# Modulation sums in PSUM: 14 instead of 5 of 24 blocks on VectorE, weight-tile halves split by VectorE and GpSimd, forget logits by chunk

## The chip, the cores and the metric

The kernel runs on one core of one Trainium2 chip. Times are device microseconds (us) of one execution of the whole program; ns is said where it is meant. Engines are called TensorE (matmuls), VectorE, ScalarE, GpSimd and SyncE (which issues the large loads). In rows of the profile they are PE (and PEld for weight loads), DVE, ACT, POOL and SP.

## What is computed

One layer of a hybrid encoder trunk, 256 positions of width 2048, batch 1. Cut to what the change touches:

```
mod = SiLU(c) @ W_ada + b_ada          # 6 sections of 2048 numbers: shift, scale, gate, twice
h   = RMSNorm(x) * (1 + scale_1) + shift_1
z   = h @ W_in                         # 5120 columns and 8 of the forget gates
y_A = gated MLP;  y_B = trailing means minus identity (windows 2, 4, 8, 16)
y_C = forgetting attention (8 heads x 128)
x   = x + gate_1 * (concat[y_A, y_B, y_C] @ W_out)
h   = RMSNorm(x) * (1 + scale_2) + shift_2
x   = x + gate_2 * MoE(h)              # 16 experts, top 1 group, top 2 experts
```

All of it is in float32. c is one vector, so mod is one row of 6 x 2048 numbers, each a sum over 2048 rows of W_ada.

## The kernel before

**Chunks and stages.** The width 2048 is 16 blocks k of 128. h and its share of z = h @ W_in are made chunk by chunk, CHUNKS = [(0, 2), (2, 2), (4, 4), (8, 4), (12, 4)], each (first block, number of blocks). A chunk is a stage: stage 0 runs from about 26 to 61 us of the profiled execution, stage 1 to 102, stage 2 to 169, stage 3 to 236 and stage 4 to 372. In a stage all columns of W_in are taken for the chunk's rows; the first chunk's result is copied into z (ScalarE, line 436), the later ones' are added to it (VectorE, line 438). Stage 4 has, between its nine weight tiles, the mixers too (gated MLP, trailing means, attention). From 372 to 501 us follows the output projection, four column blocks of W_out of 512 columns; after it come routing and the experts, to the end.

**Weight tiles.** Weights come as tiles of 1 MB through a ring of six, loaded by SyncE in the order in which the code asks for them; a step's load and its preparation are issued up to two steps (LOOK) ahead of its matmuls. W_in and W_out tiles are used in halves of 128x1024: ScalarE casts a half to a reduced type (hi, line 174), VectorE or GpSimd subtracts to get the rest (lo, line 175), and both go into one of three buffers whl. TensorE then does 24 matmuls for a half (hi by hi, lo by hi, hi by lo). A tile's result fills two of three PSUM banks pm, so the add into z must empty them soon. WSPLIT names the engine that splits the second half of a tile in each stage (the first is always VectorE's), WSO the same for W_out.

**Modulation blocks.** After the first chunk's, 24 blocks of mod are left: shift_1 and scale_1 for four chunks (M1A, M1B), shift and scale of the second sublayer (M2A, M2B), gate_1 (G1) and gate_2, four each. A block is 16 k rows by 256 or 512 columns of W_ada: two ring tiles or four, four k rows (eight at 256 columns) in a tile. There are two ways. With "P" TensorE multiplies one column of SiLU(c) by the tile, 16 matmuls in fp32 into a PSUM bank ada (ada_parts); a copy to SBUF and a few one-column matmuls then turn the row. With "V" (sum_parts) VectorE accumulates 16 products into an SBUF tile (ga, or grow for the gates), lines 290 and 292, and TensorE adds over the partitions afterwards with ones.

**Order.** The schedule is written by hand. PLAN has one list for each of the stages 0 to 3, one string for each weight tile: "n" asks for the next ring tile of the next chunk's modulation, "m" for one of the second sublayer's, a digit finishes a block (its column sums), "h" makes the next chunk's h (make_h). LAST is the same for stage 4. Stage 0 has besides band(g), which builds four masks for the trailing means, with VectorE (minimum, reciprocal at line 371, comparisons) and GpSimd (iota, products at lines 373 to 378). make_h needs the chunk's shift and scale, and stands at the end of the stage before. It also makes the forget gates' logits: per block k one matmul over the fp32 rows hf into a PSUM bank (late), the last of them after the first half-product.

Of the kernel before, what the change touches and what calls it, by code (L numbers as in the profile page):

```python
# [22 lines left out]
KD = D // 128  # L23
# [10 lines left out]
for _n, _w in (("c", 16), ("bcol", 64), ("gmix", 16), ("gffn", 16), ("wfz", 128), ("bs", 4), ("bscale", 4), ("qg", 1),  # L34
# [22 lines left out]
    ["n", "n", "n", "n0", "1h"],  # L57
    ["nnn", "n", "0n", "nnn", "1h"],
# [9 lines left out]
M1A, M1B, M2A, M2B, G1 = "PPVV", "PPPP", "PPPP", "PPPP", "PVVV"  # L68
WSPLIT, WSO = "VGGGG", "G"
# [46 lines left out]
def body(tc, x_d, prm_d, bg_d, wada_d, win_d, wout_d, egu_d, ed_d, out_d):  # L116
# [155 lines left out]
    def sum_parts(sec, k0, nk, after, eng, tile_of, bias=None):  # L272
        r = 16 // nk
        ng = KD // r
        buf = []

        def one(g):
            def prep():
                w = ada_load(sec, k0, nk, g)
                if g == 0:  # L280
                    buf.append(tile_of()[:, :128 * nk])
                return w
# [83 lines left out]
    def band(g):  # L366
        w = (2, 4, 8, 16)[g]
        rc = wk.tile([128, T], F32, name="hf")
        G.iota(rc, pattern=[[1, 256]], base=1, channel_multiplier=0, allow_small_or_imprecise_dtypes=True)
        V.tensor_scalar(rc, rc, float(w), None, op0=OP.min)  # L370
        V.reciprocal(rc, rc)
        V.scalar_tensor_tensor(rc, jp, float(w), rc, op0=OP.is_lt, op1=OP.mult)
        G.tensor_tensor(band0[:, g, :], rc, tri, op=OP.mult)
        G.tensor_tensor(band0[:, g, :128], band0[:, g, :128], ident, op=OP.subtract)
        rc = wk.tile([128, T], F32, name="hf")
# [68 lines left out]
    WS = [{"V": V, "G": G}[c] for c in WSPLIT]  # L444

    def piece(q, name):
# [8 lines left out]
        halves(win_d, WIN[q, c0], (V, WS[q]), lambda c, h: hpart(q, c, h), banks, True, True,  # L455
               lambda P: put(q, c0, P))

    def small_piece(q, c0, n):
        buf = []

        def one(a):
            def prep():
# [5 lines left out]
                split(hl[:, 0], hl[:, 1], buf[0][:, :, 512 * a:512 * a + 512], (V, WS[q])[a])  # L468
# [14 lines left out]
    def col_mod(sec, i, chunk, gain=None, eng=None):  # L483
# [15 lines left out]
        return steps(sum_parts(sec, k0, nk, after_sum, eng, lambda: wk.tile([128, 512], F32, name="ga", bufs=2)))  # L499
# [12 lines left out]
    def forget_a():  # L512
        fs = wk.tile([128, 256], F32, name="hf")
# [137 lines left out]
    def pool_mix():  # L651
        bsc = par("bscale")
        ds_ = []
        for g in range(5):
            if g < 4:
# [4 lines left out]
                d = wk.tile([128, 256], F32, name="hf")  # L660
# [159 lines left out]
    WO = (V, {"V": V, "G": G}[WSO])  # L820
# [67 lines left out]
    def g1_steps(n):  # L888
# [6 lines left out]
        return steps(sum_parts(2, 4 * n, 4, lambda a: None, ENG(G1[n]), lambda: r4s[n], n))  # L895
# [509 lines left out]
```

## Time and profile before

| | |
|---|---|
| median of 3 runs | 1456.18 us (1456.14 to 1457.46) |
| the profiled execution | 1460.89 us, its span 1459.1 us |
| mean granted TensorE clock | 0.958 |
| TensorE busy | 1264.6 us, 87% of the span |
| VectorE busy | 693.5 us, 48% |
| ScalarE busy | 412.8 us, 28% |
| GpSimd busy | 146.0 us, 10% |
| moved by DMA | 539.14 MB, 369 GB/s |

The span is what the trace covers, 1.8 us less than the execution's own time. Busy shares are means over stages that differ: GpSimd's 146 us all lie in the first 501 us. In rows of groups, `xN` is the number of instructions, then come the busy time in us and the mean of one in ns, then the idle time of the engine just ahead of them and what ended most of it. In rows of the timeline the first number is the start, the second the length, and brackets say how long the engine had been idle and for what.

### The profile page before, as it was taken

What the parts mean: (1) busy time and instruction counts of PE and PEld (TensorE: products, weight loads), DVE (VectorE), ACT (ScalarE), POOL (GpSimd) and SP (SyncE); (2) the same over time, 40 slices, a digit from 0 to 9 for tenths busy, and PEclk for the clock granted to TensorE, in tenths of its full rate; (3) what the DMA queues carried; (4) which work ended last, traced back from release to release, by engine and by line L of the source; (5) the groups of instructions that cost most, each with busy time, mean ns of one, the idle gap of its engine ahead of it and who ended that gap; (6) DMA issues with size and microseconds to landing.
All of it is one profiled execution on the core that took longest, in us unless ns stands there. A gap on an engine that the chain in (4) does not pass through costs nothing.

```text
span 1459.1 us, 17581 instructions
## 1 busy us (share of the span) xinstructions
PE 1264.6 (87%) x6930; PEld 703.1 (48%) x6930; DVE 693.5 (48%) x1184; ACT 412.8 (28%) x720; POOL 146.0 (10%) x89
## 2 busy tenths in 40 slices
PE   5999999999989997999968999789997879858865
PEld 3666666666667563575324753337633222222221
DVE  3757483555798372795125961169711202202112
ACT  4433333646333240583003840028400000000000
POOL 0423332311333100000000000000000000000000
PEclk8999999999999998999999999999999999979988
DMA  9787787888877868998999989999899999999997
GB/s 378 270 348 281 281 340 265 303 351 328 349 278 270 310 288 367 427 428 317 421 426 427 426 318 419 424 428 426 333 408 428 427 426 427 428 426 428 426 426 303
DMA packets 49207, 539.14 MB, mean 369 GB/s; under 512 B 5464, under 2 KB 5592, under 8 KB 7008
## 3 DMA queue, kind: packets, MB, share of 16 engines
q1 hardware_dynamic: 47664, 534.79, 89.7%
q10 hardware_dynamic: 1456, 3.17, 0.6%
q8 instruction: 56, 0.92, 0.2%
q14 instruction: 31, 0.25, 0.0%
HBM read 535.85 MB, written 2.10 MB: 369 GB/s over the span
## 4 chain that ended last, share of the span: by engine, by line
PE 38%; DMA 27%; DVE 5%; issue 1%; ACT 1%; DVEq 0%; ACTq 0%
PE lbank L170 28%; DMA ring<-in_e_down_dram 11%; DMA ringl<-in_e_gu_dram 9%; DMA ring<-in_e_gu_dram 7%; PE bank L170 5%; PE pm L170 3%; DVE grow L292 2%; PE ada L170 1%; DVE whl L175 1%; DVE el L175 1%; ACT el L174 0%; DVE grow L290 0%; PE lgp L170 0%; DVE hid L1225 0%; PE pt L170 0%
## 5 line engine op out<-in xcount | busy, mean ns | idle before, releaser
L170 PE MATMUL pm<-whl,hT 128*128 128x512 f32 x1120 | 300.9, 405 | 19.9 <-DVE whl L175 10.8
L170 PEld LDWEIGHTS pm<-whl,hT 128*128 128x128 f32 x1120 | 212.3, 193 | 93.6 <-issue 15.3
L170 PE MATMUL lbank<-ringl,xr 128*32 128x256 f32 (+1 forms) x1152 | 143.7, 496 | 38.0 <-DMA ringl<-in_e_gu_dram 37.8
L170 PE MATMUL lbank<-el,xs 128*128 128x512 f32 x576 | 139.9, 401 | 10.2 <-ACT el L174 7.4
L170 PE MATMUL lbank<-ring,xr 128*32 128x256 f32 (+1 forms) x864 | 105.6, 491 | 34.1 <-DMA ring<-in_e_gu_dram 34.0
L174 ACT CAST whl<-ring 128x1024 fp32r<-128x1024 f32 x96 | 99.0, 1048 | 125.7 <-PE pm L170 70.7
L175 POOL TENSOR_TENSOR whl<-ring,whl 128x1024 fp32r<-128x1024 f32 x43 | 108.3, 2518 | 231.7 <-ACT whl L174 211.0
L170 PEld LDWEIGHTS lbank<-el,xs 128*128 128x128 f32 x576 | 109.3, 192 | 41.0 <-ACT el L174 10.6
L170 PE MATMUL bank<-y,gt 128*128 128x512 f32 x240 | 119.1, 619 | 0.0
L1284 DVE TENSOR_TENSOR xa<-xa,bank 128x512 f32<-128x512 f32 x120 | 82.5, 687 | 69.9 <-PE bank L170 69.9
L170 PEld LDWEIGHTS lbank<-ringl,xr 128*32 128x32 f32 (+1 forms) x1152 | 51.9, 128 | 129.8 <-issue 68.5
L170 PE MATMUL lbank<-ring,hidT 128*64 128x512 f32 (+1 forms) x576 | 103.8, 624 | 11.5 <-DMA ring<-in_e_down_dram 11.5
L1275 DVE TENSOR_TENSOR y<-lbank,g2w 128x512 f32<-128x512 f32 x60 | 41.5, 691 | 145.7 <-PE lbank L170 145.7
L174 ACT CAST el<-ring 128x512 fp32r<-128x512 f32 x144 | 89.7, 623 | 29.6 <-PE lbank L170 21.7
L175 DVE TENSOR_TENSOR el<-ring,el 128x512 fp32r<-128x512 f32 x144 | 92.7, 688 | 0.0
L175 DVE TENSOR_TENSOR whl<-ring,whl 128x1024 fp32r<-128x1024 f32 x53 | 72.2, 1368 | 35.9 <-ACT whl L174 33.6
L170 PE MATMUL ada<-ring,cact 128*1 128x512 f32 (+1 forms) x648 | 75.1, 566 | 15.6 <-DMA ring<-in_w_ada_dram 14.4
L1171 ACT COPY gt<-bank 128x256 f32<-128x256 f32 x15 | 5.6, 372 | 287.9 <-PE bank L1169 287.9
L170 PEld LDWEIGHTS lbank<-ring,xr 128*32 128x32 f32 (+1 forms) x864 | 39.5, 128 | 98.4 <-DMA ring<-in_e_gu_dram 48.4
L1225 DVE TENSOR_TENSOR hid<-hid,lbank 128x512 f32<-128x512 f32 x12 | 8.2, 687 | 165.0 <-PE lbank L170 164.7
L170 PE MATMUL lbank<-el,hidT 128*128 128x512 f32 x288 | 74.8, 411 | 12.2 <-DVE el L175 8.3
L438 DVE TENSOR_TENSOR z<-z,pm 128x512 f32<-128x512 f32 x72 | 49.0, 685 | 71.8 <-PE pm L170 71.8
(363 smaller groups left out, 1219.3 us busy)
## 6 DMA issues: line engine op xcount, KB each, us to landing
ringl<-in_e_gu_dram SPq DMA_DIRECT2D x60, 2048.0 KB, 20.1
ring<-in_w_ada_dram SPq DMA_DIRECT2D x90, 1024.0 KB, 7.0
ring<-in_e_gu_dram SPq DMA_DIRECT2D x45, 2048.0 KB, 24.4
ring<-in_e_down_dram SPq DMA_DIRECT2D x45, 2048.0 KB, 25.6
ring<-in_w_in_dram SPq DMA_DIRECT2D x35, 1024.0 KB, 7.0
ringm<-in_e_gu_dram SPq DMA_DIRECT2D x15, 2048.0 KB, 21.7
ringm<-in_e_down_dram SPq DMA_DIRECT2D x15, 2048.0 KB, 21.5
ring<-in_w_out_dram SPq DMA_DIRECT2D x12, 1024.0 KB, 8.3
```

The costliest lines, as they stand in the source:

```text
L170: E.matmul(out, lhsT=lhsT, rhs=rhs, start=start, stop=stop, skip_group_check=True)
L174: S.copy(hi, src)
L175: (eng or V).tensor_tensor(lo, src, hi.bitcast(F32), op=OP.subtract)
L292: eng.scalar_tensor_tensor(a, w[:, j, :], ck, a, op0=OP.mult, op1=OP.add)
L438: V.tensor_tensor(dst, dst, P[h], op=OP.add)
L1171: S.copy(gt, p[:, :256])
L1225: V.tensor_tensor(hid[:, o], hid[:, o], P[2 * b + 1], op=OP.mult)
L1275: V.tensor_tensor(y, P, g2w[:, c0:c0 + 512], op=OP.mult)
L1284: V.tensor_tensor(a, a, p, op=OP.add)
```

## The change

Nine more blocks go from "P" to "V": shift_1 and scale_1 for chunk 1, scale_1 for chunks 3 and 4, the second sublayer's shift entirely, and shift_1 for chunk 2 (of 24 blocks 14 are then VectorE's, two of the nine are 256 columns wide). The partial sums now lie in the PSUM bank ada that the "P" way uses; only the last of 16 operations writes to an SBUF tile. Every first half of a weight tile is split by VectorE and every second half by GpSimd; before, this held everywhere but in stage 0, where VectorE did both. The forget logits of a chunk are all issued behind the first half-product. The tile hf gets five buffers instead of two, and PLAN asks for the next chunk's modulation earlier.

```diff
@@
 PLAN = [
-    ["n", "n", "n", "n0", "1h"],
-    ["nnn", "n", "0n", "nnn", "1h"],
+    ["nn", "nn", "0", "", "1h"],
+    ["nn", "nn", "nn0", "nn", "1h"],
     ["n", "n", "nm", "nn", "n", "n", "n", "0m", "1h"],
     ["mn", "n", "n", "n", "n", "nn", "n0", "m", "1h"],
 ]
@@
-M1A, M1B, M2A, M2B, G1 = "PPVV", "PPPP", "PPPP", "PPPP", "PVVV"
-WSPLIT, WSO = "VGGGG", "G"
+M1A, M1B, M2A, M2B, G1 = "VVVV", "VPVV", "VVVV", "PPPP", "PVVV"
+WSPLIT, WSO = ["VG", "VG", "VG", "VG", "VG"], "VG"
@@
-    def sum_parts(sec, k0, nk, after, eng, tile_of, bias=None):
+    def sum_parts(sec, k0, nk, after, acc, eng, tile_of, bias=None):
         r = 16 // nk
         ng = KD // r
+        P = accs[acc][:, :128 * nk]
...
             def run(w):
-                a = buf[0]
                 for j in range(r):
                     k = r * g + j
                     ck = cact[:, k:k + 1]
                     if k == 0:
-                        eng.tensor_scalar(a, w[:, j, :], ck, None, op0=OP.mult)
+                        eng.tensor_scalar(P, w[:, j, :], ck, None, op0=OP.mult)
+                    elif k < KD - 1:
+                        eng.scalar_tensor_tensor(P, w[:, j, :], ck, P, op0=OP.mult, op1=OP.add)
                     else:
-                        eng.scalar_tensor_tensor(a, w[:, j, :], ck, a, op0=OP.mult, op1=OP.add)
+                        a = tile_of()[:, :128 * nk]
+                        eng.scalar_tensor_tensor(a, w[:, j, :], ck, P, op0=OP.mult, op1=OP.add)
@@
-        rc = wk.tile([128, T], F32, name="hf")
+        rc = wk.tile([128, T], F32, name="hf", bufs=5)
@@ def make_h(q):
-            if late is not None:
-                late()
-
-            def late(k=k, t=t):
+            ts.append((k, t))
+
+        def late():
+            for k, t in ts:
                 o = 32 * (k % 4)
                 mm(fzp[o:o + 8, :], wfz[:, k, :], t, start=k < 4, stop=k >= KD - 4)
         todo.insert(1, (late, None, False)) if todo else late()
@@
-    WS = [{"V": V, "G": G}[c] for c in WSPLIT]
+    WS = [[{"V": V, "G": G}[c] for c in x] for x in WSPLIT]
```

How this moves instructions is seen in the program's order on VectorE and GpSimd. Names are those of the tiles (out<-in), L175 is the split, and xN stands for N alike in a row; line numbers are each kernel's own (L287 and L289 of the changed kernel are the sums in PSUM).

VectorE in stage 0 before, from its first weight tile on: both halves of two ring tiles, then a band's four operations, then splits again.

```order
L175 TENSOR_TENSOR whl<-ring_65,whl 128x1024 x2
L175 TENSOR_TENSOR whl<-ring_63,whl 128x1024 x2
L370 TENSOR_SCALAR hf<-hf 128x256
L371 RECIPROCAL hf<-hf 128x256
L372 SCALAR_TENSOR_TENSOR hf<-jp,hf 128x256
L376 TENSOR_SCALAR hf<-jp 128x128
L175 TENSOR_TENSOR whl<-ring_64,whl 128x1024 x2
```

The same place after:

```order
L175 TENSOR_TENSOR whl<-ring_65,whl 128x1024
L175 TENSOR_TENSOR whl<-ring_63,whl 128x1024
L370 TENSOR_SCALAR hf<-hf 128x256
L371 RECIPROCAL hf<-hf 128x256
L372 SCALAR_TENSOR_TENSOR hf<-jp,hf 128x256
L376 TENSOR_SCALAR hf<-jp 128x128
L287 TENSOR_SCALAR ada_108<-ring_65,cact 128x256
L289 SCALAR_TENSOR_TENSOR ada_108<-ring_65,cact,ada_108 128x256 x7
L289 SCALAR_TENSOR_TENSOR ada_108<-ring_63,cact,ada_108 128x256 x7
L292 SCALAR_TENSOR_TENSOR ga<-ring_63,cact,ada_108 128x256
L175 TENSOR_TENSOR whl<-ring_65,whl 128x1024
```

The second halves have left VectorE, and the 16 operations of a block stand between a band and the next split.

GpSimd in stage 0 after, from the first second half on (before, the four bands' rows stood in a row here, and no split of stage 0):

```order
L175 TENSOR_TENSOR whl<-ring_65,whl 128x1024
L369 IOTA hf 128x256
L373 TENSOR_TENSOR band_134<-hf,tri 128x256
L374 TENSOR_TENSOR band_134<-band_134,ident 128x128
L377 TENSOR_TENSOR band_135<-hf,tri 128x128
L378 TENSOR_TENSOR band_135<-band_135,ident 128x128
L175 TENSOR_TENSOR whl<-ring_63,whl 128x1024
```

A second half's split now stands behind a band's four products on GpSimd.

VectorE in stage 4 before, around the first half of the seventh weight tile: the split follows ylo (a gated MLP result) directly.

```order
L175 TENSOR_TENSOR ylo<-pt_114,hT_124 128x256
L175 TENSOR_TENSOR whl<-ring_63,whl 128x1024
L324 TENSOR_TENSOR mod<-ada_108,prm_69 128x4
L325 SCALAR_TENSOR_TENSOR mod<-mod,prm_69 128x4
L438 TENSOR_TENSOR z<-z,pm 128x512 x2
```

The same place after:

```order
L175 TENSOR_TENSOR ylo<-pt_114,hT_124 128x256
L287 TENSOR_SCALAR ada_109<-ring_65,cact 128x512
L289 SCALAR_TENSOR_TENSOR ada_109<-ring_65,cact,ada_109 128x512 x3
L175 TENSOR_TENSOR whl<-ring_63,whl 128x1024
L324 TENSOR_TENSOR mod<-ada_108,prm_69 128x4
L325 SCALAR_TENSOR_TENSOR mod<-mod,prm_69 128x4
L289 SCALAR_TENSOR_TENSOR ada_109<-ring_65,cact,ada_109 128x512 x4
L289 SCALAR_TENSOR_TENSOR ada_109<-ring_63,cact,ada_109 128x512 x4
L438 TENSOR_TENSOR z<-z,pm 128x512 x2
```

One tile's sum of a second-sublayer block stands ahead of the split now, two more ahead of the adds into z.

## Rows read from the trace of the kernel before

**Rows 1.** Windows: length; busy PE, PEld, DVE, ACT, POOL (count); granted clock, DMA share, GB/s.

```profile
26.00:61.00 35.00, 32.73 (x183) 23.35 (x182) 24.54 (x31) 21.19 (x32) 10.01 (x16) 0.95 0.86 326
61.00:102.00 41.00, 39.48 (x203) 25.14 (x204) 21.71 (x30) 11.12 (x13) 14.82 (x9) 0.96 0.75 292
...
236.00:372.00 136.00, 131.47 (x783) 85.11 (x782) 72.44 (x173) 72.42 (x194) 29.69 (x22) 0.99 0.80 304
372.00:501.00 129.00, 117.60 (x569) 88.80 (x568) 92.66 (x87) 43.80 (x62) 45.46 (x20) 0.95 0.78 299
501.00:1459.00 958.00, 805.24 (x4510) 386.01 (x4510) 390.12 (x726) 212.52 (x361) 0.00 (x0) 0.95 0.96 401
```

**Rows 2.** Timeline of TensorE in stage 2: start, length, operation.

```profile
147.40 1.04 PE L170 MATMUL ada<-ring,cact 128*1 128x512 f32 x8
148.37 5.73 PE L170 MATMUL pm<-whl,hT 128*128 128x512 f32 x24
```

**Rows 3.** Groups of VectorE over the whole program, forms apart.

```profile
L175 DVE TENSOR_TENSOR whl<-ring,whl 128x1024 fp32r<-128x1024 f32 x53 | 72.2, 1368 | 35.9 <-ACT whl L174 33.6 <-POOL whl L175 2.2
...
L438 DVE TENSOR_TENSOR z<-z,pm 128x512 f32<-128x512 f32 x72 | 49.0, 685 | 71.8 <-PE pm L170 71.8
...
L292 DVE SCALAR_TENSOR_TENSOR grow<-ring,cact,grow 128x512 f32<-128x512 f32 x33 | 35.3, 1069 | 1.0
...
L585 DVE SCALAR_TENSOR_TENSOR s<-pt,Fq,maskb 128x256 f32<-128x256 f32 x5 | 2.4, 476 | 0.0
```

**Rows 4.** Timeline of VectorE and GpSimd in the output projection.

```profile
417.29 3.10 DVE L292 SCALAR_TENSOR_TENSOR grow<-ring,cact,grow 128x512 f32<-128x512 f32 x4
...
421.15 3.20 POOL L175 TENSOR_TENSOR whl<-ringm,whl 128x1024 fp32r<-128x1024 f32 x1 [5.46 <-ACT whl L174]
...
422.04 5.22 DVE L292 SCALAR_TENSOR_TENSOR grow<-ring,cact,grow 128x512 f32<-128x512 f32 x4
```

**Rows 5.** TensorE's waits, 372 to 470 us, and its timeline around them.

```profile
PE pm L170 <- DVE xg L839: 7.0, 3, 3.1
...
404.39 0.50 PE L170 MATMUL pm<-whl,hT 128*128 128x512 f32 x1 [1.27 <-DVE xg L839]
...
434.87 0.72 PE L170 MATMUL pm<-whl,hT 128*128 128x512 f32 x1 [2.70 <-DVE xg L839]
435.39 0.63 PE L170 MATMUL pm<-whl,ylo 128*128 128x512 f32 x1
...
438.86 0.39 PE L170 MATMUL pm<-whl,ylo 128*128 128x512 f32 x1
```

**Rows 6.** Timeline of stage 0 on ScalarE, VectorE and TensorE.

```profile
35.26 0.58 ACT L436 COPY z<-pm 128x512 f32<-128x512 f32 x1 [0.72 <-PE pm L170]
...
38.28 1.75 DVE L371 RECIPROCAL hf<-hf 128x256 f32<-128x256 f32 x1
...
40.07 0.42 DVE L372 SCALAR_TENSOR_TENSOR hf<-jp,hf 128x256 f32<-128x256 f32 x1
...
60.89 1.16 PE L170 MATMUL pt<-diag,xa 128*128 128x128 f32 x8 [0.96 <-DVE mod L320]
```

**Rows 7.** GpSimd: a split in the timeline of stage 2, and the bands' groups.

```profile
152.55 2.40 POOL L175 TENSOR_TENSOR whl<-ring,whl 128x1024 fp32r<-128x1024 f32 x1 [4.23 <-ACT whl L174]
...
L374 POOL TENSOR_TENSOR band<-band,ident 128x128 f32<-128x128 f32 x4 | 4.4, 1106 | 0.3
...
L373 POOL TENSOR_TENSOR band<-hf,tri 128x256 f32<-128x256 f32 x4 | 2.9, 734 | 24.6 <-DVE hf L372 24.6
```

**Rows 8.** VectorE's waits, 236 to 372 us (total us, times, longest), and its timeline.

```profile
DVE z L438 <- PE pm L170: 21.1, 13, 4.4
...
DVE qk L571 <- ACT qk L570: 6.6, 6, 4.2
...
245.51 0.69 DVE L438 TENSOR_TENSOR z<-z,pm 128x512 f32<-128x512 f32 x1 [3.52 <-PE pm L170]
...
256.84 0.69 DVE L438 TENSOR_TENSOR z<-z,pm 128x512 f32<-128x512 f32 x1 [4.38 <-PE pm L170]
```

More of the change, by code (lines that the diff above doesn't have):

```diff
@@ L278, in prep @@
             def prep():
[L279 to L282, printed above, removed]
+                return ada_load(sec, k0, nk, g)
             def run(w):
-                a = buf[0]
                 for j in range(r):
@@ L374, in band @@
         G.tensor_tensor(band0[:, g, :128], band0[:, g, :128], ident, op=OP.subtract)
-        rc = wk.tile([128, T], F32, name="hf")
+        rc = wk.tile([128, T], F32, name="hf", bufs=5)
         V.tensor_scalar(rc[:, :128], jp[:, :128], float(w), 1.0 / w, op0=OP.is_lt, op1=OP.mult)
@@ L388, in make_h @@
         hq = hbuf(q)
-        late = None
+        ts = []
         for c in range(nk):
@@ L394, in make_h @@
                 mm(p[:, 128 * h:128 * h + 128], xa[:, h, 128 * k:128 * k + 128], diag[:, h, :])
-            t = wk.tile([128, T], F32, name="hf")
+            t = wk.tile([128, T], F32, name="hf", bufs=5)
             V.tensor_scalar(t, p[:, :T], mod[:, 1, k:k + 1], mod[:, 0, k:k + 1], op0=OP.mult, op1=OP.add)
             split(hq[:, 0, c, :], hq[:, 1, c, :], t)
-            if late is not None:
-                late()
-            def late(k=k, t=t):
+            ts.append((k, t))
+        def late():
+            for k, t in ts:
                 o = 32 * (k % 4)
@@ L453, in banks @@
             return P
-        halves(win_d, WIN[q, c0], (V, WS[q]), lambda c, h: hpart(q, c, h), banks, True, True,
+        halves(win_d, WIN[q, c0], WS[q], lambda c, h: hpart(q, c, h), banks, True, True,
                lambda P: put(q, c0, P))
@@ L467, in prep @@
                 hl = hp.tile([128, 2, 2, 512], F32R, name="whl")
-                split(hl[:, 0], hl[:, 1], buf[0][:, :, 512 * a:512 * a + 512], (V, WS[q])[a])
+                split(hl[:, 0], hl[:, 1], buf[0][:, :, 512 * a:512 * a + 512], WS[q][a])
                 return hl
@@ L498, in col_mod @@
             return steps(ada_parts(sec, k0, nk, after, 0 if sec < 2 else 1))
-        return steps(sum_parts(sec, k0, nk, after_sum, eng, lambda: wk.tile([128, 512], F32, name="ga", bufs=2)))
+        return steps(sum_parts(sec, k0, nk, after_sum, 0 if sec < 2 else 1, eng, lambda: wk.tile([128, 512], F32, name="ga", bufs=2)))
     for f in col_mod(0, 0, CHUNKS[0]) + col_mod(1, 1, CHUNKS[0], "gmix"):
@@ L512, in forget_a @@
     def forget_a():
-        fs = wk.tile([128, 256], F32, name="hf")
+        fs = wk.tile([128, 256], F32, name="hf", bufs=5)
         V.tensor_copy(fs, fzp)
@@ L659, in pool_mix @@
                 mm(p[:, 128:256], z[:, 1, c0:c0 + 128], band1[:, g, :], start=False)
-                d = wk.tile([128, 256], F32, name="hf")
+                d = wk.tile([128, 256], F32, name="hf", bufs=5)
                 V.tensor_copy(d, p[:, :256])
@@ L818, in body @@
     V.tensor_scalar(limR, capR, -1.0, 512.0, op0=OP.mult, op1=OP.add)
-    WO = (V, {"V": V, "G": G}[WSO])
+    WO = [{"V": V, "G": G}[c] for c in WSO]
     def wout_steps(n, Ps):
@@ L894, in g1_steps @@
             return steps(ada_parts(*gate_args(2, n, r4s[n])))
-        return steps(sum_parts(2, 4 * n, 4, lambda a: None, ENG(G1[n]), lambda: r4s[n], n))
+        return steps(sum_parts(2, 4 * n, 4, lambda a: None, n % 2, ENG(G1[n]), lambda: r4s[n], n))
     r4s = []
```

## Prediction, made before the changed kernel ran

> **What bounds the kernel now.** I read the busy time by stage first [rows 1]. In the five chunk stages (26 to 372 us) TensorE is busy 93 to 97% of the time (stage 0: 32.73 of 35 us; stage 4: 131.47 of 136), while VectorE has between 10 and 64 us free per stage. In the stretch from 372 to 501 us, the output projection, TensorE drops to 117.60 of 129. After 501 us come routing and experts; nothing there is edited, and it begins when the part before it is done. So the change is worth what it moves the end of the first 501 us; the last 958 us are carried along.
>
> TensorE's rhythm in a chunk stage is seen in the timeline [rows 2]: 24 matmuls of a weight tile take 5.73 us, and one tile of a modulation block 1.04 us, overlapping its neighbours by some 0.07. Two other readings matter. The accumulator sum of a block that VectorE does already runs at 3.10 us for 4 operations when nothing disturbs it, 0.775 us each, and at 5.22 us for 4 when GpSimd's split of a weight tile runs at the same moment [rows 4]. And at the boundary between two column blocks of the output projection TensorE stands 2.70 us behind VectorE; over three such boundaries 7.0 us [rows 5].
>
> **The change, step by step.**
>
> *Price of one sum operation in PSUM.* The trace has no accumulation into PSUM. Nearest rows [rows 3]: a 512-wide add with one PSUM input takes 685 ns (z adds, 72 of them), with nothing that depends on it next: the lower bound, 0.69. A 256-wide scalar_tensor_tensor takes 476 ns with a PSUM input and 0.42 without [rows 3, 6], so PSUM adds 0.05. On 0.775 this gives 0.83 us, which I take: 3.3 us for a tile of 4, and 0.56 for the 256-wide operations of stage 0. Upper bound: the mean of the present sums with GpSimd's blocking in it, 1069 ns [rows 3], if PSUM does not free them of it. That it does is my reading of the 72 z adds: their mean equals an undisturbed add, though GpSimd works in the same stages; the splits without a PSUM operand average 1368 ns.
>
> The Trainium skill says the same in "SBUF — State Buffer", Who interferes with whom: the pair of SBUF ports that VectorE shares with GpSimd is locked for a whole instruction, and a VectorE instruction with at most one SBUF input, outside the two-port modes, doesn't need it. The trace agrees (5.22 against 3.10 for two SBUF inputs, 685 ns for one); by this rule the sums cost no more than the undisturbed price.
> Against the change speaks "Perfetto Trace Analysis", Optimizing Scalar/DVE Operations: an access costs VectorE about 60 ns in SBUF and 125 in PSUM. By that an operation would take 0.84 instead of 0.83 (an estimate from that page), and the total below would rise by 1 to 2 us; the 0.05 us of the rows is a little less.
>
> *What TensorE loses.* Nine more blocks leave it: seven with 4 tiles of about 0.95 us, two with 2 tiles of 1.04, together 31 us. That is the gain if nothing else becomes late.
>
> *Stage 0.* It gets both 256-wide blocks: 32 operations of 0.56 us, 18 us. VectorE had 10 us free, and gives 5 us of splits to GpSimd. But its order is now fixed as split, band, 16 sums, split, band, 16 sums, split, split. The first split of this chain follows ScalarE's cast, which now stands behind all four copies of the first tile (the last copy ended at 35.26 + 0.6 [rows 6]): it runs from 36.9 to 38.1. Then band 2.7 (the 1.75 us reciprocal is most of it [rows 6]), sums 9.0, split 1.2, band 2.7, sums 9.0, split 1.2: 63.9 us. Only now is the first half of the fourth tile ready, and three halves of 2.9 us remain for TensorE: 72.6, then column sums. Before, the stage's h began at 60.89 [rows 6]. **+12 us.** On GpSimd each second half's split now stands behind four band products (0.73, 1.1 and two smaller ones) that wait for VectorE's reciprocal, and takes 2.40 us itself [rows 7]: the second tile's second half is ready only at about 45, the third's at 58. TensorE waits there too, but these waits lie inside the VectorE chain just counted.
>
> *Stage 1.* Eight sums (6.6 us) now stand between a tile's split and the adds that empty its PSUM banks; with three banks TensorE can start just one more half-product. A cycle is split 1.2, sums 6.6, add 0.7, product 1.45, add 0.7: 10.7 us for a tile that took about 7. Two such tiles, +8, less 4 us of modulation matmuls: **+4**.
>
> *Stages 2 and 3.* Nine tiles, ten sum tiles each. A tile costs VectorE 1.2 + 1.4 + 3.3 = 5.9 us against TensorE's 5.73; two tiles carry a double sum (9.2). The gain of 5 to 6 us of modulation matmuls, of the 1 us that the forget matmuls no longer stand ahead of the first product, and of two present waits is eaten by these: **-1** together.
>
> *Stage 4.* Twelve sum tiles, 40 us, all after 264 us. VectorE's idle time there that TensorE causes can take them: z adds 21.1 us less the 9.2 before the first sum (four waits, the two long ones in [rows 8]), query/key transposes 6.6, and some 4 in smaller waits, 22 us. Its waits for ScalarE's exponentials and roots stay, since they are links of the same chain. So VectorE ends 40 - 22 = 18 us later, though TensorE has 11 us less to do. One sum tile stands directly ahead of the seventh tile's split, for which TensorE waits at 305 us already without slack. I take **+17**.
>
> *Output projection.* Three blocks were summed in SBUF at 1069 ns and more. Per column block VectorE now needs 4 splits (4.9), 16 sums (13.3), bias, copy and three x updates (3.9): 22 us, below TensorE's 26 of work. The period was 30.4. The waits of 7.0 us go, as do a little over 1 us each of matmuls slowed after them (0.63 instead of 0.39 us behind the 2.70 us gap [rows 5]): **-10**.
>
> GpSimd's four more splits (10 us) lie inside stage 0's chain. More buffers for the h rows and the earlier loads cost nothing: DMA is 75 to 86% busy in these stages [rows 1].
>
> Sum: 12 + 4 - 1 + 17 - 10 = +22 us. The profiled execution took 1460.9 us (span 1459.1); the same on it is 1483. The median of the runs is 1456.2, 4.7 less, so **1478 us** is forecast.
>
> **The rivals.**
> *VectorE's idle time takes the sums (faster).* If TensorE's order leaves VectorE enough time in stage 4, because it runs ahead of TensorE at each split, the 17 turn into minus 11, TensorE's share: 1478 - 28 = 1450. For it: 64 us free there [rows 1]. Against: a tile is placed ahead of a split or an add that is needed next, and the seventh split has no slack. It decides if splits of stage 4 still come before TensorE needs them. 15%.
> *The PSUM sum is as cheap as an add (0.69).* 0.14 us less on 32 + 16 + 48 operations of stages 0, 1 and 4 is 13 us, and stages 2 and 3 become TensorE's again, -7: 1458. 11%; with the first rival too, 1430, 5%.
> *PSUM does not free the sums of GpSimd's lock* (or accumulating there is slow): 1.07 instead of 0.83 on about 156 operations on the path, +37, and the 10 of the output projection do not come: 1525. Against it stand the 72 undisturbed adds. 7%.
> *As forecast:* 62%, with 1466 to 1490 as its own range.
>
> **How the numbers follow.** About 0.2% is what a measurement of this kernel can tell from no change, 1453 to 1459. Slower: the forecast 62, the lock 7, a third of the cheap sum: 72%. Same: half of the cheap sum, 5%. Faster: idle time 15, both 5, the rest of the cheap sum: 23%. The range reaches to the idle-time case below, 1450, and above beyond the forecast's own 1490 towards the lock, to 1502; outside lie the half of the idle-time case, most of the lock and the case with both.
>
> **What would show it.** Right: h of chunk 1 begins near 73 us instead of 60.89, h of the later chunks near 118, 184 and 251; TensorE's gaps in stage 0 end at VectorE's and GpSimd's splits; scalar_tensor_tensor into ada at 0.83 us, also while GpSimd splits; in stage 4 gaps of several us at the seventh and ninth split; a column block of the output projection every 26 us. Wrong: sum operations near 0.69 or over 1.0; stage 4 shorter than 125 us; TensorE above 95% busy in stage 0. The step I trust least is stage 4, which rests on counted idle time instead of a chain.

## The result, and the profile after

The changed kernel takes 1493.18 us (median of 4 runs, 1491.67 to 1505.02) against 1456.8 us before (4 runs beside it): 1.0267 times as long, 95% interval 1.0215 to 1.032. It is slower, as forecast, but by 36 us where 22 were forecast. Its profiled execution took 1491.67 us, with a span of 1489.5.

The windows of the changed kernel, cut where TensorE begins the next chunk's h, where it meets the first matmul with ylo (start of the output projection), and where the routing begins. Chunk 1's h has two blocks, and where stage 0 has the new list TensorE makes the first, then waits for VectorE: there the cut is at the second block (in the changed kernel at 74.13 us, the first block at 69.81). Columns as in [rows 1].

```profile
20.70:74.00 53.30, 38.83 (x134) 28.37 (x133) 35.59 (x63) 21.57 (x31) 20.03 (x22) 0.81 0.72 288
74.00:120.00 46.00, 36.25 (x165) 24.24 (x165) 32.27 (x47) 10.52 (x12) 11.11 (x8) 0.93 0.61 233
120.00:185.40 65.40, 57.88 (x258) 46.27 (x257) 57.66 (x79) 20.01 (x22) 24.49 (x10) 0.95 0.82 312
185.40:254.00 68.60, 56.33 (x258) 43.67 (x257) 61.98 (x77) 20.09 (x22) 21.70 (x10) 1.00 0.75 285
254.00:416.60 162.60, 134.80 (x689) 94.13 (x689) 107.62 (x224) 71.21 (x191) 29.11 (x23) 0.85 0.71 266
416.60:531.60 115.00, 110.66 (x552) 84.44 (x554) 75.81 (x84) 41.87 (x59) 43.09 (x20) 0.99 0.84 328
531.60:1489.00 957.40, 807.85 (x4528) 384.86 (x4520) 390.37 (x730) 214.04 (x363) 0.00 (x0) 0.95 0.96 402
```

The same cuts in the kernel before, for the three parts that moved most.

```profile
22.00:60.90 38.90, 36.45 (x196) 25.70 (x196) 26.22 (x35) 21.93 (x33) 10.25 (x17) 0.91 0.87 334
...
235.80:372.30 136.50, 131.97 (x785) 85.53 (x785) 72.84 (x174) 72.72 (x194) 30.14 (x23) 0.99 0.81 304
372.30:499.00 126.70, 115.30 (x552) 87.28 (x554) 91.44 (x84) 41.93 (x59) 45.16 (x20) 0.95 0.78 298
```

Stage by stage, with the lengths of the other windows of before (40.8, 67.1 and 67.0 us for stages 1 to 3):

| part | forecast | measured |
|---|---|---|
| stage 0 | +12 | +14.4 (38.9 to 53.3) |
| stage 1 | +4 | +5.2 (40.8 to 46.0) |
| stages 2 and 3 | -1 | -0.1 (134.1 to 134.0) |
| stage 4 | +17 | +26.1 (136.5 to 162.6) |
| output projection | -10 | -11.7 (126.7 to 115.0) |
| ahead of stage 0, and from routing on | 0 | -3.5 |
| span | +22 | +30.4 (1459.1 to 1489.5) |

The medians differ by 6 us more than the spans, because the profiled execution of before was 4 us above its median and that of the changed kernel the fastest of its four. What the reader is to see in the windows: the granted clock. In stage 4 it is 0.85 where it was 0.99, in stage 0 0.81 where it was 0.91. TensorE is busy for 134.80 us of stage 4 with 689 matmuls, and was for 131.97 with 785: fewer matmuls, more time. Twelve tiles of 8 matmuls left it, at 0.97 us each (147.40 to 148.37 in [rows 2]); at the old speed 120.3 us would remain, so 14.5 us are slower matmuls. The idle time rose from 4.5 to 27.8 us. Together 14.5 + 23.3 - 11.6 is the 26. Of the 27.8 us TensorE waits 20.2 for VectorE's last sums (ga), splits (whl), queries and keys (qk): the three rows below (us, times, longest), and 1.7 us more for qk.

```profile
PE ada L170 <- DVE ga L292: 7.5, 2, 5.2
PE pm L170 <- DVE whl L175: 6.5, 2, 3.3
PE ada L170 <- DVE qk L571: 4.5, 1, 4.5
```

Stage 0 reads the same way. TensorE's idle time there rose from 2.5 to 14.5 us, and its waits are:

```profile
PE pm L170 <- POOL whl L175: 5.3, 2, 2.7
PE pm L170 <- ACT whl L174: 3.9, 3, 1.6
PE pt L170 <- DVE mod L324: 3.6, 1, 3.6
PE pm L170 <- DVE whl L175: 1.6, 3, 0.5
```

Its matmuls are slower here too. Four modulation tiles of 1.04 us (0.97 without the overlap) left it, so 32.6 of the 36.45 busy us would remain at the old speed, and it is busy for 38.83: some 6 us more.

TensorE's timeline in stage 4 shows where its matmuls get slower there; the window of 16 us around the first gap has a mean granted clock of 0.70.

```profile
318.00:334.00 16.00, 9.63 (x47) 7.06 (x40) 14.85 (x29) 4.54 (x10) 4.38 (x3) 0.70 0.70 264
```

```profile
325.96 1.22 PE L170 MATMUL pm<-whl,hT 128*128 128x512 f32 x2 [1.73 <-ACT whl L174]
330.46 7.28 PE L170 MATMUL pm<-whl,hT 128*128 128x512 f32 x22 [3.28 <-DVE whl L175]
...
345.90 1.89 PE L170 MATMUL ada<-ring,cact 128*1 128x512 f32 x8 [5.21 <-DVE ga L292]
...
377.10 7.82 PE L170 MATMUL pm<-whl,hT 128*128 128x512 f32 x22 [3.24 <-DVE whl L175]
```

VectorE around the first of these gaps:

```profile
325.36 0.74 DVE L287 TENSOR_SCALAR ada<-ring,cact 128x512 f32<-128x512 f32 x1
326.14 2.34 DVE L289 SCALAR_TENSOR_TENSOR ada<-ring,cact,ada 128x512 f32<-128x512 f32 x3
328.38 2.02 DVE L175 TENSOR_TENSOR whl<-ring,whl 128x1024 fp32r<-128x1024 f32 x1
```

The gap at the seventh tile's split is the forecast one: four sum operations, then a split, and TensorE gets its rest of the half 4.5 us after its first two matmuls. Two things were not forecast. The 22 matmuls behind the gap take 7.28 and 7.82 us, where all 24 of such a half took 5.73 [rows 2], and 8 matmuls of a modulation tile 1.89 instead of 1.04. And at 345.90 TensorE waits 5.21 us for VectorE's last sum (ga) before it may start a block of its own: the sums and TensorE's next block use the same PSUM bank.

VectorE's groups over the whole program, which answer to [rows 3]:

```profile
L289 DVE SCALAR_TENSOR_TENSOR ada<-ring,cact,ada 128x512 f32<-128x512 f32 x159 | 120.0, 754 | 4.7
...
L289 DVE SCALAR_TENSOR_TENSOR ada<-ring,cact,ada 128x256 f32<-128x256 f32 x28 | 13.7, 490 | 1.0
```

A sum operation in PSUM takes 0.754 us, and 0.490 at 256 columns. With what lies between them, as the forecast counted, four take 3.12 us (at 428.49) where it had 3.3, and 14 of 256 columns 7.31 us, 0.52 each where it had 0.56. That is no more than undisturbed ones in SBUF, 3.10 us for four in [rows 4]. None of the 196 accumulations in PSUM takes over 0.757 us; of the 75 in SBUF in the kernel before, the median takes 0.752 and the longest 2.96.

### The profile page after: what moved, and what is told of

The parts are those of the page before. It is cut to its first block, busy times and chain, and to the rows that moved or that the text cites. A ratio compares the mean times of both kernels' runs of the same rounds, so it can differ in the third digit from the quotient of the medians.

```text
span 1489.5 us, 17147 instructions
## 1 busy us (share of the span) xinstructions
PE 1249.9 (84%) x6642; PEld 708.5 (48%) x6642; DVE 766.6 (51%) x1324; ACT 408.4 (27%) x711; POOL 150.1 (10%) x93
## 4 chain that ended last, share of the span: by engine, by line
PE 56%; DMA 25%; DVE 12%; issue 3%; ACT 2%; POOL 1%; SPq 0%; DVEq 0%; POOLq 0%; ACTq 0%
PE lbank L170 28%; PE pm L170 16%; DMA ring<-in_e_down_dram 10%; DMA ring<-in_e_gu_dram 7%; DMA ringl<-in_e_gu_dram 7%; PE bank L170 5%; DVE ada L289 4%; PE ada L170 3%; DVE whl L175 3%; PE pt L170 2%; DMA ring<-in_w_ada_dram 1%; DVE z L438 1%; DVE el L175 1%; ACT whl L174 0%; DVE hf L371 0%
## 5 line engine op out<-in xcount | busy, mean ns | idle before, releaser
L170 PE MATMUL pm<-whl,hT 128*128 128x512 f32 x1120 | 314.1, 419 | 52.4 <-DVE whl L175 31.4
L170 PEld LDWEIGHTS pm<-whl,hT 128*128 128x128 f32 x1120 | 221.5, 202 | 119.2 <-DVE whl L175 40.7
L170 PE MATMUL lbank<-el,xs 128*128 128x512 f32 x576 | 136.7, 395 | 9.9 <-ACT el L174 6.9
L175 POOL TENSOR_TENSOR whl<-ring,whl 128x1024 fp32r<-128x1024 f32 x47 | 115.6, 2460 | 275.5 <-ACT whl L174 215.2
L289 DVE SCALAR_TENSOR_TENSOR ada<-ring,cact,ada 128x512 f32<-128x512 f32 (+1 forms) x187 | 133.7, 715 | 5.6
L175 DVE TENSOR_TENSOR el<-ring,el 128x512 fp32r<-128x512 f32 x144 | 92.7, 688 | 0.0
L175 DVE TENSOR_TENSOR whl<-ring,whl 128x1024 fp32r<-128x1024 f32 x49 | 77.4, 1582 | 28.5 <-ACT whl L174 28.4
```

Source lines behind the costliest of these rows:

```text
L170: E.matmul(out, lhsT=lhsT, rhs=rhs, start=start, stop=stop, skip_group_check=True)
L175: (eng or V).tensor_tensor(lo, src, hi.bitcast(F32), op=OP.subtract)
L289: eng.scalar_tensor_tensor(P, w[:, j, :], ck, P, op0=OP.mult, op1=OP.add)
```

## The experiments

Each was timed beside runs of the kernel before, whose medians were 1458.1, 1459.8 and 1459.0 us beside the three sets of four. Ratios are to these, with a 95% interval; they are not quotients of two medians, and differ from those by up to 0.25%. Lengths of stages come from one profiled execution of each kernel, and most are good to 2 or 3 us: the projection of the same code took 126.7 and 124.3 us in two kernels, and 115.0 and 117.6 in two others.

**Stage 0 without sums.** Chunk 1's two blocks go back to TensorE.

```diff
-M1A, M1B, M2A, M2B, G1 = "VVVV", "VPVV", "VVVV", "PPPP", "PVVV"
+M1A, M1B, M2A, M2B, G1 = "PVVV", "PPVV", "VVVV", "PPPP", "PVVV"
```

> The changed kernel with the two 256-wide blocks of chunk 1 back on TensorE (M1A PVVV, M1B PPVV), all else as changed, so stage 0 has no sums on VectorE. Order theory (the sums stand in VectorE's order ahead of splits that TensorE waits for): chunk 1's h, at 74 us in the changed kernel, begins at 62 to 66 us and the kernel takes 1481 to 1485 us instead of 1493. Second-half theory (GpSimd's splits behind the bands are what makes stage 0 late): chunk 1's h still begins after 71 us, 1490 to 1493 us. If both, something between.

Measured: 1506.07 us (1497.47 to 1509.3), ratio 1.0319 (1.0279 to 1.0358). Stage 0 is as late as with the sums; TensorE's waits in it (us, times, longest) and the timeline of one tile:

```profile
21.20:77.00 55.80, 39.87 (x199) 28.12 (x198) 20.35 (x32) 22.13 (x33) 21.22 (x22) 0.88 0.72 276
```

```profile
PE pm L170 <- POOL whl L175: 9.1, 2, 5.1
PE pt L170 <- DVE mod L324: 3.8, 1, 3.8
```

```profile
34.96 1.23 DVE L175 TENSOR_TENSOR whl<-ring,whl 128x1024 fp32r<-128x1024 f32 x1 [8.52 <-ACT whl L174]
...
36.43 1.75 DVE L371 RECIPROCAL hf<-hf 128x256 f32<-128x256 f32 x1
...
38.73 0.73 POOL L373 TENSOR_TENSOR band<-hf,tri 128x256 f32<-128x256 f32 x1 [9.75 <-DVE hf L372]
...
40.89 2.34 POOL L175 TENSOR_TENSOR whl<-ring,whl 128x1024 fp32r<-128x1024 f32 x1
...
43.28 4.14 PE L170 MATMUL pm<-whl,hT 128*128 128x512 f32 x10 [4.01 <-POOL whl L175]
...
47.94 2.00 ACT L174 CAST whl<-ring 128x1024 fp32r<-128x1024 f32 x2
49.03 1.23 DVE L175 TENSOR_TENSOR whl<-ring,whl 128x1024 fp32r<-128x1024 f32 x1 [10.25 <-ACT whl L174]
```

So my order theory fails here: without any sum, a loop goes from VectorE's band over GpSimd's band products, its split (2.34 us), TensorE, ScalarE's copies and its next cast back to VectorE, 14.1 us a round (from the split at 34.96 to the one at 49.03). In the changed kernel the same two splits stand at 33.44 and 47.24, 13.8 us apart, and VectorE, done with its sums, waits 1.73 us for the cast ahead of the second. Stages 2 and 3, whose code is that of the changed kernel, took 9.5 us more in this run (143.5 us, at granted clocks of 0.95 and 0.93 where the changed kernel had 0.95 and 1.00); why is open, and the kernel's time is therefore not used for stage 0.

**Stage 0 without GpSimd's splits.**

```diff
-WSPLIT, WSO = ["VG", "VG", "VG", "VG", "VG"], "VG"
+WSPLIT, WSO = ["VV", "VG", "VG", "VG", "VG"], "VG"
```

> The changed kernel with both halves of stage 0's tiles split by VectorE again (WSPLIT of stage 0 VV), sums as changed. Order theory: VectorE's chain gets four splits of 1.22 us more, chunk 1's h begins at 75 to 79 us instead of 74 and the kernel takes 1494 to 1498 us. Second-half theory: h begins at 62 to 68 us and the kernel takes 1481 to 1487 us.

Measured: 1503.18 us (1496.75 to 1507.66), ratio 1.0314 (1.0275 to 1.0353).

```profile
22.40:79.00 56.60, 40.74 (x133) 29.55 (x133) 39.94 (x67) 21.57 (x31) 10.30 (x17) 0.79 0.65 257
```

The first block of h is made at 74.67 and the second at 79.16, after a start 1.7 us later than the changed kernel's. That is close to the order theory's 75 to 79 us; the kernel's time is some 5 us above its range. Here the chain through VectorE's sums is the long one. Either is enough, and to undo one alone brings nothing.

**Stage 0's list of the plan, undone and done alone.** First the changed kernel with the old list, then the kernel before with the new one.

```diff
-    ["nn", "nn", "0", "", "1h"],
+    ["n", "n", "n", "n0", "1h"],
```

> The changed kernel with only stage 0's list of the plan as before (n, n, n, n0, 1h: one modulation tile behind each weight tile instead of two behind the first two). Sums on VectorE and second halves on GpSimd stay. With two modulation tiles between weight tiles, two steps of lookahead are used up by them, so a weight tile's cast stands behind the copies of the tile before. Lookahead theory (this closes a loop of cast, split, band, GpSimd's split, matmuls, copies, and each of sums and second halves only lengthens it): chunk 1's h at 63 to 68 us instead of 74, kernel 1483 to 1488 us instead of 1493. Two-loop theory (sums on VectorE, or second halves on GpSimd, are each enough by themselves): h still after 71 us, 1490 to 1497 us.

> The kernel before with only stage 0's list of the plan changed to nn, nn, 0, empty, 1h. No sums on VectorE in stage 0, both halves split by VectorE. Lookahead theory: TensorE waits once a tile for the cast behind the copies, but its two modulation tiles lie in part of that wait: chunk 1's h at 63 to 67 us instead of 61, kernel 2 to 8 us slower than before, ratio 1.002 to 1.006. Two-loop theory: nothing to see, h at 60 to 62 us and the ratio within 0.998 to 1.002. If the lookahead is all of it: h after 70 us, ratio above 1.007.

Measured: the changed kernel with the old list 1492.88 us (1489.88 to 1494.81), ratio 1.0204 (1.0174 to 1.0235); the kernel before with the new list 1467.2 us (1463.59 to 1469.35), ratio 1.004 (1.0018 to 1.0062). Stage 0 of the one and of the other:

```profile
22.30:73.70 51.40, 35.25 (x129) 25.23 (x130) 35.15 (x62) 21.48 (x31) 21.30 (x25) 0.87 0.61 236
```

```profile
22.50:67.70 45.20, 38.09 (x197) 26.15 (x197) 25.63 (x36) 22.11 (x33) 14.75 (x18) 0.88 0.85 327
```

The new list costs 6.3 us of stage 0 by itself (38.9 to 45.2), and not by the lookahead alone: TensorE waits 4.3 us for mod at the end of the stage (1.0 before) and 2.2 us for VectorE's splits (0.5 before). VectorE is late with mod because a band stands ahead of it, and the band waits 3.9 us for GpSimd's iota, which stands behind GpSimd's first split of stage 1. The same wait for mod is in the changed kernel (3.6 us) and in the two experiments above. To give the changed kernel the old list brings 1.9 us only (53.3 to 51.4): there VectorE's sums of half a block stand ahead of its splits (TensorE waits 11.0 us for them, in four waits). So stage 0 has three costs that overlap, and the two-loop theory holds for the changed kernel.

**Stage 4 without sums.**

```diff
-M1A, M1B, M2A, M2B, G1 = "VVVV", "VPVV", "VVVV", "PPPP", "PVVV"
+M1A, M1B, M2A, M2B, G1 = "VVVV", "VPVV", "PPPP", "PPPP", "PVVV"
```

> The changed kernel with the second sublayer's shift back on TensorE (M2A PPPP), so that stage 4 has no sum tile on VectorE. Order theory: stage 4, 162.6 us in the changed kernel against 136.5 before, falls to 136 to 142 us, the kernel takes 1467 to 1474 us, and the granted clock of stage 4, 0.85 in the changed kernel, is above 0.95 again, since it fell only behind TensorE's gaps. Idle-time theory (VectorE had room for these sums, and stage 4 is long for another reason: the forget matmuls, the hf buffers, a clock that falls by itself): stage 4 stays above 155 us and its clock below 0.9; 1486 to 1493 us, or more, since TensorE gets 11 us of work back.

Measured: 1469.01 us (1467.07 to 1473.38), ratio 1.008 (1.0048 to 1.0111).

```profile
255.00:389.70 134.70, 130.42 (x785) 85.07 (x785) 72.93 (x174) 72.62 (x194) 30.12 (x23) 0.99 0.83 315
```

The kernel's time is as expected. Stage 4 is at 134.7 us, just below what was expected, and its clock at 0.99, though TensorE has its 11 us of work again. All of stage 4's loss is that of these sums.

**TensorE's gaps in stage 4 filled.** The matmuls added read the identity and write columns of a bank that nothing reads.

```diff
+    def fill(n):
+        for _ in range(n):
+            mm(dum, ident, ident)
@@ ada_parts, run
+                if sec == 4 and k0 > 4 and g == 0:
+                    fill(20 if k0 == 8 else 9)
@@ halves, run (gap: seventh and ninth tile of stage 4)
+                        if gap and a + c + h == 0:
+                            fill(7)
+                            mm(P[h], xh, hl[:, 0, c, :], first, False)
+                            mm(P[h], xl, hl[:, 0, c, :], False, False)
+                            fill(14)
+                            mm(P[h], xh, hl[:, 1, c, :], False, False)
+                            continue
```

> The changed kernel with 71 extra matmuls of 128 columns on TensorE (about 0.22 us each, 15 us in all, into unused columns of a PSUM bank, nothing reads them), placed where TensorE stands in stage 4: ahead of and within the first half of the seventh and ninth weight tile, and ahead of two blocks of the second sublayer's scale. Clock theory (TensorE's granted clock falls behind these gaps, and the slower matmuls behind them are 10 us or more of stage 4's loss): 22 matmuls behind the gap take 5.3 to 5.8 us instead of 7.3 and 7.8, a modulation tile 1.04 instead of 1.9, the clock of stage 4 rises from 0.85 to over 0.93, and the kernel gets 4 to 10 us faster, 1483 to 1489 us, though TensorE has more to do. Rival (VectorE's chain sets the end of stage 4 and the slow matmuls are hidden behind it): the matmuls get faster but stage 4 keeps its 162 us within 2, 1491 to 1496 us.

Measured: 1485.42 us (1481.59 to 1492.52), ratio 1.0169 (1.0133 to 1.0206). The window of stage 4, and TensorE's timeline at the seventh and ninth tile and at the block that waited 5.21 us:

```profile
254.35:407.20 152.85, 140.19 (x832) 104.17 (x831) 107.22 (x224) 71.25 (x191) 29.21 (x23) 0.96 0.75 283
```

```profile
331.08 5.29 PE L170 MATMUL pm<-whl,hT 128*128 128x512 f32 x22
...
339.52 4.63 PE L170 MATMUL lgp<-ident 128*128 128x128 f32 x40
344.77 1.04 PE L170 MATMUL ada<-ring,cact 128*1 128x512 f32 x8 [0.62 <-DVE ga L300]
...
371.50 5.32 PE L170 MATMUL pm<-whl,hT 128*128 128x512 f32 x22 [0.62 <-DVE whl L175]
```

With more to do, TensorE ends stage 4 9.7 us sooner (162.6 to 152.9). The 22 matmuls take 5.29 and 5.32 us, the clock is 0.96. Of the 140.19 busy us the filling takes 19.9 (six rows of the timeline, in which each of the 71 stands as two), which leaves 120.3, as worked out above for the old speed. The clock theory holds, with the kernel 7.8 us faster, and some 10 us of stage 4's loss are the clock behind the gaps.

**PSUM alone, and PSUM for the gates alone.** The kernel before with sum_parts of the changed kernel (all five blocks in PSUM), then with the two blocks of stages 2 and 3 left in SBUF.

```diff
-                        eng.scalar_tensor_tensor(a, w[:, j, :], ck, a, op0=OP.mult, op1=OP.add)
+                        eng.scalar_tensor_tensor(P, w[:, j, :], ck, P, op0=OP.mult, op1=OP.add)
```

> The kernel before with nothing changed but the accumulation of its five VectorE blocks in PSUM instead of SBUF. PSUM theory (sums in SBUF lose time to GpSimd's splits, and in the output projection TensorE waits for them): an operation takes about 0.75 us instead of 1.07, the output projection falls from 126.7 to 114 to 117 us, and the kernel takes 1444 to 1449 us, ratio 0.992 to 0.995. Rival (the output projection is shorter in the changed kernel for another reason, such as fewer matmuls or another order): the operation gets cheaper, but the projection stays above 123 us and the ratio within 0.998 to 1.002.

> The kernel before with PSUM sums for the three gate blocks of the output projection alone; the two blocks in stages 2 and 3 stay in SBUF. If the wait of 5.0 us and the slower matmuls behind it in stage 2 of the kernel with all five in PSUM (74.6 us instead of 67) come from the shared bank, since TensorE's next block needs the bank in which VectorE still sums: stage 2 takes 66 to 68 us, the projection 115 to 118 us, and the kernel 1443 to 1449 us, ratio 0.990 to 0.994. If they come from something else: stage 2 stays above 72 us and the ratio at 0.995 to 0.998.

Measured: all five 1450.53 us (1447.09 to 1462.54), ratio 0.9958 (0.9937 to 0.9978); the gates alone 1449.32 us (1446.57 to 1450.38), ratio 0.991 (0.9888 to 0.9932). With all five in PSUM, stage 2 and TensorE's longest wait there:

```profile
99.90:174.50 74.60, 67.40 (x307) 47.40 (x306) 40.33 (x55) 20.77 (x23) 22.74 (x10) 0.93 0.78 304
```

```profile
PE ada L170 <- DVE ga L292: 5.0, 1, 5.0
```

With the gates alone, stage 2 and the projection:

```profile
98.60:165.70 67.10, 63.31 (x306) 44.81 (x306) 41.76 (x55) 20.58 (x23) 22.48 (x10) 1.00 0.84 336
...
369.20:486.90 117.70, 113.33 (x552) 86.46 (x554) 75.89 (x85) 41.82 (x59) 43.06 (x20) 0.96 0.83 321
```

The projection's gain is the PSUM sums', by themselves: 126.7 to 117.7 us, and TensorE's waits there for VectorE's last adds (xg) fall from 7.0 to 1.4 us. With all five the kernel was a little slower than the PSUM theory had it. The 7.5 us of stage 2 are the price of the shared bank (4.2 of them slower matmuls: TensorE is busy for 67.40 instead of 63.24 us), and go when the block there is in SBUF. But the block of stage 3 lost nothing by the bank: that stage took 63.7 us with its sums in PSUM and 66.9 with them in SBUF. The version with the gates alone is faster than both kernels, by 0.9% of the ratio and 0.7% of the medians.

**All sums in SBUF.** The changed kernel with an SBUF tile in place of the bank (three tiles ga instead of two).

```diff
-        P = accs[acc][:, :128 * nk]
+                a = P = buf[0]
```

> The changed kernel with all 14 blocks summed in an SBUF tile instead of PSUM (three such tiles instead of two). Port theory (PSUM frees the sums of GpSimd's splits): an operation of 512 columns takes 0.95 to 1.1 us on average instead of 0.75, the output projection 125 to 128 us instead of 115, and the kernel 1503 to 1518 us. Bank theory (the shared bank's waits of TensorE, 7.5 us in stage 4, weigh as much as the cheaper operation): stage 4 gets 5 us or more shorter than 162, the kernel 1492 to 1500 us.

Measured: 1525.27 us (1522.21 to 1530.48), ratio 1.0453 (1.0418 to 1.0487).

```profile
L293 DVE SCALAR_TENSOR_TENSOR ga<-ring,cact,ga 128x512 f32<-128x512 f32 x126 | 111.7, 886 | 3.7
...
L293 DVE SCALAR_TENSOR_TENSOR grow<-ring,cact,grow 128x512 f32<-128x512 f32 x33 | 37.2, 1129 | 1.0
...
L293 DVE SCALAR_TENSOR_TENSOR ga<-ring,cact,ga 128x256 f32<-128x256 f32 x28 | 20.7, 738 | 1.0
...
L295 DVE SCALAR_TENSOR_TENSOR ga<-ring,cact,ga 128x256 f32<-128x256 f32 x2 | 1.0, 485 | 0.1
```

An operation of 512 columns takes 0.886 and 1.129 us in the two large groups (0.96 over all 180, 173.2 us), and 0.738 at 256 columns where an undisturbed one takes 0.485. The price is the port theory's. The projection, 123.7 us, is below that theory's range and the kernel's time above it: every stage got longer than in the changed kernel, stage 0 to 60.0 and stage 4 to 164.9 us. The bank theory falls. In stage 4 TensorE still waits 7.7 us for last sums (ga), now at the column sums, so its waits at the bank in the changed kernel show VectorE's lateness; what the bank costs there beyond that is not shown.

**Sums spread.** The 16 operations of a block of the second sublayer's shift are not done at their turn, but one behind each step of the queue, into an SBUF tile.

```diff
+    pend = deque()
+    def drip(n=1):
+        for _ in range(min(n, len(pend))):
+            pend.popleft()[1]()
@@ run_first
         f(x) if x is not None else f()
+        drip()
@@ sum_parts, run
+                if sec == 3:
+                    for j in range(r):
+                        pend.append((slots[g], lambda j=j: late_op(w, j, r * g + j)))
+                    return
```

> The changed kernel with the sums of the second sublayer's shift not issued four at a time at their turn, but one operation behind each step that is taken from the queue (and at the latest before their ring tile is loaded again, or their block is finished), into an SBUF tile, so that TensorE's next block need not wait for the bank. The same 48 operations and the same TensorE work in stage 4. Place theory (what costs is that four operations stand ahead of a split or of the bank's release): the splits of the seventh and ninth tile are not late, stage 4 takes 140 to 152 us instead of 162 and the kernel 1478 to 1485 us. Volume theory (VectorE has no room for 48 operations in this stage, wherever they stand): stage 4 stays above 157 us, 1488 to 1498 us.

Measured: 1523.87 us (1521.22 to 1529.83), ratio 1.0433 (1.0395 to 1.0471); stage 4 takes 178.3 us. TensorE's waits there:

```profile
PE pt L179 <- DVE ga L294: 25.5, 2, 18.0
PE ada L179 <- DVE ga L294: 10.4, 1, 10.4
...
PE pm L179 <- DVE whl L184: 1.1, 2, 0.5
```

Neither theory's time came, though stage 4 is longer than 157 us, as the volume theory has it. It is 15.7 us longer than in the changed kernel, about half of what the kernel lost. The splits are no longer late (1.1 us, where two waits of 3.3 and 3.2 us stood), but the column sums of a block stayed at their place in TensorE's order, and now wait up to 18 us for sums that were put off. The edit moved the wait from one consumer to another. It also made the sums dearer, since they lie in SBUF: 0.892 us on average. Whether the sums would fit with the column sums put off too was not tried and stays open.

**Stage 0 and stage 4's sums undone together.** Stage 0 as before in all three respects, M2A on TensorE.

```diff
-    ["nn", "nn", "0", "", "1h"],
+    ["n", "n", "n", "n0", "1h"],
-M1A, M1B, M2A, M2B, G1 = "VVVV", "VPVV", "VVVV", "PPPP", "PVVV"
-WSPLIT, WSO = ["VG", "VG", "VG", "VG", "VG"], "VG"
+M1A, M1B, M2A, M2B, G1 = "PVVV", "PPVV", "PPPP", "PPPP", "PVVV"
+WSPLIT, WSO = ["VV", "VG", "VG", "VG", "VG"], "VG"
```

> The changed kernel with stage 0 as before (its list of the plan, both halves split by VectorE, chunk 1's blocks on TensorE) and the second sublayer's shift on TensorE. What stays of the change: PSUM sums, three more blocks of chunks 2 to 4 on VectorE, the forget logits, the buffers. If stage 0 and the second sublayer's shift hold the whole loss (about 15 and 24 us of the changed kernel's 36), the kernel takes 1451 to 1459 us, ratio 0.994 to 1.000: the output projection gives 9 us, stage 1 costs 5. If something else of the change costs too, above 1462 us, ratio over 1.002.

Measured: 1451.44 us (1448.47 to 1454.69), ratio 0.9932 (0.9904 to 0.996). Stage 1 of it:

```profile
59.00:105.90 46.90, 38.60 (x168) 25.90 (x169) 33.16 (x46) 10.63 (x12) 13.43 (x9) 0.89 0.72 273
```

Stage 0 is at 36.8 us, stage 4 at 136.3, the projection at 115.0; stage 1 keeps its 46.9. The two parts hold the whole loss, and more, and the time lies at the lower end of what was expected.

**Forget logits alone.** The kernel before with make_h of the changed kernel and five buffers hf.

> The kernel before with only the forget logits of a chunk issued behind the first half-product, and five buffers of hf instead of two. My step put 1 us on it in stages 2 and 3: chunk h in 4.05 to 4.2 us instead of 4.6, ratio 0.998 to 1.000. Rival: the four matmuls, now together in one place, cost there what they gave, ratio 0.9995 to 1.001; this can't be told from no change by the time, only by the rows.

Measured: 1455.25 us (1450.43 to 1463.85), ratio 0.9979 (0.9955 to 1.0002): not told apart from no change. The rows show the step: in stage 2 the first product begins 3.15 us behind the chunk's first block of h (100.50 to 103.65) instead of 4.55 (101.65 to 106.20), and the logits then take 0.62 us behind the first half-product. Stages 2 and 3 together are 1.2 us shorter than before, but stage 2 is 0.3 us longer (67.4) and stage 3 1.5 us shorter (65.5), so that the microsecond of the step reached the end of a stage is not shown.

## Why the prediction was right in direction and too small

**The price of a sum** was set at 0.83 us and measured 0.78 by the same reading (four in 3.12 us): PSUM cost nothing on top. That it frees the sums of GpSimd's splits was right: 0.754 or 0.755 us in every kernel with PSUM sums, 0.886 to 1.440 in the groups of 512 columns where the changed kernel sums in SBUF; the projection's 9 us in the kernel before follow from it. This is the Trainium skill's rule on the shared ports ("SBUF — State Buffer", Who interferes with whom), and the runs agree. The higher access time in PSUM that the Trainium skill states ("Perfetto Trace Analysis", Optimizing Scalar/DVE Operations) doesn't show here: 0.490 us in PSUM beside 0.485 in SBUF at 256 columns, 0.754 beside a median of 0.752 at 512.

**Output projection, -10**: -11.7, and -9.0 where PSUM sums were put into the kernel before alone. Right, by its mechanism too: the waits named there fell from 7.0 to 1.4 us.

**Stage 0, +12**: +14.4, right in size by luck and wrong in its cause. The step that failed reads that TensorE's waits for GpSimd's halves "lie inside the VectorE chain just counted". They are a loop of their own, as long as VectorE's: with the sums gone, stage 0 took 55.8 us, with GpSimd's splits gone 56.6, against 53.3. Only with both gone did it fall, to 45.2 (the kernel before with the new list), and to 38.9 with the old list. Two costs stood in no term: the wait for mod, 3.6 us, and some 6 us of slower matmuls. The last tile's matmuls end at 69.6 us, ahead of the forecast's 72.6; the wait for mod then takes the stage past it.

**Stage 1, +4**: +5.2, and TensorE waits 5.7 us in two waits for the adds into z, as the mechanism named has it (sums between a split and the adds); no run took these sums out alone. Of the five parts it is the only one much longer than before in the last but one experiment. **Stages 2 and 3, -1**: -0.1, the balance of two larger terms. Twelve tiles left TensorE there, 11.6 us where the forecast writes 5 to 6, which holds for one of the two stages; and its waits for VectorE's splits rose from 6.5 to 18.1 us.

**Stage 4, +17**: +26.1. The place was right (the seventh and ninth split, and TensorE's 11 us go for nothing); the term was mis-sized, because VectorE's lateness was taken as all of it. Two costs were missing. TensorE's matmuls are slower behind the gaps: 14.5 us of its busy time, of which the filled gaps gave 9.7 back to the end of the stage. And its next block waits for the bank: 7.5 us in two waits, the same wait as in stage 2 with PSUM alone, though with the sums in SBUF TensorE waits as long for them (7.7 us). Against them the sums were cheaper by 0.05 us each, some 2 us on 48.

Of the rivals, the cheaper sum came true in part (0.78, between 0.69 and 0.83), but without the gain that I gave it: the chain that it should have shortened in stage 0 was not set by the sums alone. That VectorE's idle time would take the sums did not happen. That stage 0 and stage 4 are the whole loss was tested by undoing both: 41.7 us of the 1493.2 went, where the two terms add up to 40.5. In the prediction's chances the case "faster" adds up to 22, not 23.

## What to carry to other kernels

Before work is moved from the busy engine to an idler one, count each loop that passes through the places where it lands, not the longest alone: two that are equally long hide each other, and undoing either shows nothing. Price a wait of TensorE by the matmuls behind it too, since the gaps of a few us here were followed by a lower granted clock, and look whom a shared accumulator bank makes wait. The part worth keeping here is the smallest: the sums of three gate blocks moved to PSUM, 0.9% faster, beside a change that costs 2.7%.

## What the runs showed of the hardware that was not expected

An in-place accumulation by VectorE in PSUM costs what an undisturbed one in SBUF does (0.754 and 0.752 us at 512 columns, 0.490 and 0.485 at 256), and GpSimd's splits did not lengthen it. The gaps of 3 to 5 us in TensorE's stream in stage 4 were followed by matmuls at about half speed (8 in 1.89 us instead of 1.04, so by their length at the lower of the clock's two levels, 1.2 instead of 2.4 GHz), and filling it with useless matmuls made the kernel faster. And the bias operation of a gate block, 8 partitions by 512 columns, took 0.74 us in SBUF before and 2.15 on average in the kernels whose sums are in PSUM:

```profile
468.96 2.40 POOL L175 TENSOR_TENSOR whl<-ring,whl 128x1024 fp32r<-128x1024 f32 x1 [5.74 <-ACT whl L174]
...
469.15 2.75 DVE L295 SCALAR_TENSOR_TENSOR grow<-bgt,ident,grow 8x512 f32<-8x512 f32 x1
```

It still has its inputs in SBUF, and it is now the one that meets GpSimd's split: in the changed kernel all three overlap one and end 0.5 us behind it (here the split ends at 471.36 and the operation at 471.90), and in the kernel before none of the three overlaps one.
